# Encoder layer in fp32 on one core: merged products taken by pairs, cached rows on GpSimd's queue, a written order for the first up products, last hidden rows kept in the ring tiles, and new places in SBUF for the operands

## The chip, the core and the metric

The kernel runs on one core of a Trainium2 chip. The metric is the device time of one execution in microseconds, lower is better. The five engines are named as the profile names them: PE (TensorE, its weight loads shown as PEld), DVE (VectorE), ACT (ScalarE), POOL (GpSimd) and SP (SyncE). SP does nothing but start DMAs; POOL starts DMAs too, on a queue of its own.

## What is computed

One inference step of a one-layer encoder, all in fp32, for 1024 new frames and 64 frames of a running stream with 512 cached key and value rows (1088 tokens of 1024 features together).

```python
def mixer(xn, ...):
    cb, cc, ch, q, k, v, ga, gb = jnp.split(xn @ w_in, splits, axis=-1)   # 1024 -> 5120
    cv, conv_state = causal_conv(cc * ch, conv_prefix, w_conv)           # width 3
    ya = (cb * cv) @ w_conv_out                                          # 512 -> 1024
    o, new_k, new_v = attn_fn(heads(q), heads(k), heads(v))              # 8 heads of 64, own chunk + 8 before
    yb = o.reshape(B, L, ATT_DIM) @ w_attn_out                           # 512 -> 1024
    merged = jax.nn.sigmoid(ga) * ya + jax.nn.sigmoid(gb) * yb
    return merged @ w_out, conv_state, new_k, new_v                      # 1024 -> 1024

def trunk(x, ...):
    x = x + mixer(rmsnorm(x, g_mix), ...)
    x = x + (silu(xf @ w_ff1) * (xf @ w_ff3)) @ w_ff2    # xf = rmsnorm(x, g_ffn); 1024 -> 2816 -> 1024
    return rmsnorm(x, g_final), conv_state, new_k, new_v
```

Outputs are the two y, the new convolution states, and the key and value caches, of which `cache_k_sample` and `cache_v_sample` are the old cache moved up by 64 rows with the 64 new rows behind.

## The kernel before

**Products.** Every fp32 operand is split into a high and a low part in the type fp32r: ACT casts the high part, DVE subtracts it from the source to get the low part (`split`, lines 122 and 123). A product is then three matmuls into one PSUM bank: high weight by high data, high weight by low data, low weight by high data. Tokens are two halves of 544 (`HT`), each taken in two pieces of 272 columns (`HN`).

**Seven products for a 2x2 block.** The input projections for q, k, the convolution (cc, ch, cb) and half of gb, and the FFN's up projections, run in units of 256 output columns (`Unit`, `run`). A unit replaces the eight block products of a 2x2 by 2x2 block product by seven, in the order of `STEPS` (1, 2, 6, 7, 5, 4, 3), each 24 matmuls of 128x272 on line 240. Steps 1, 2, 4, 3 use a quarter of the normalized tokens (tiles `xn`, later `mg`), steps 6, 7, 5 use sums of quarters (tiles `xs`, later `tt`). The weights' sums are made on DVE (line 197). Two units run interleaved with each other, step by step: `run` is a generator, and after each step it prepares a later unit's weights.

**Stages, in order of time.** (1) Load, RMSNorm and transpose the tokens tile by tile; V is projected on the way (lines 475 to 477, tokens as weights, 512 columns moving). (2) Projection units to 300 us or so. The epilogues run on ACT and DVE and use one big scratch tile `scr`, cut by hand into slots that are handed out in turn (`slot(STAGE, ...)`, `slot(CC, ...)`, `slot(UT, ...)`). `cc_done` and its inner `whole` (line 543) add a unit's parts out of PSUM, `summed` (line 551) does so for the others. `cache_load` brings cached k and v rows to `scr`, and `cache_tile` stores them back into the sample caches, splits v into `v_d` (`put_v`), and transposes k. `bias_tables` (lines 117 and 118) copies a table through a `STAGE` slot. (3) Gates ga and gb (lines 302 to 304 of `product`), with the attention's heads woven in between; `gate` copies the result to a tile `gst` (line 779) and POOL stores it to DRAM (line 780). (4) For each of eight blocks m of 128 output rows: `ya` from the tile `u` and `yb` from the tile `ob`, each 48 matmuls; `ob` is made from the attention's output at the same time (line 1015 multiplies by the row factor, then `split`). (5) Output projection w_out (lines 1084 to 1089), RMSNorm, transposes (line 1153) and the sums `tt` (`second_half`, line 1179). (6) 22 up units a0, b0, a1, b1 and so on, with SiLU and the product in `hidden_done`; `keep` splits seven forms of a hidden block into a tile `hq` and POOL stores it to `h_d` (line 1245). (7) Down projection (line 1526): hidden rows come back as weights (`ht`), w_ff2 lies split in seven `ring` tiles and is the 512 columns wide moving operand. (8) Final norm and the stores.

**What sets the order.** A tile framework schedules each engine's instruction list ahead of time from the program and from estimated costs; `tc.issue_after(x)` keeps what is written in its block behind instruction x. On the chip each engine takes its list strictly in order.

**Where operands lie.** Tiles are placed one behind the other in each partition of SBUF, so sizes decide places. Before, a token tile is `[P, 2, 4, HT]`: all four high blocks, then all four low ones. Worked out from the sizes, the 272 columns wide moving operands start 32 bytes past a multiple of 64 in `xn`, `mg` and `tt` (6000 matmuls) and on a multiple of 64 in `xs`, `u` and `ob` (1632). The weights of all of them start 224 bytes past a multiple of 256.

Of the kernel before, what the change touches and what calls it, by code (L numbers as in the profile page):

```python
# [15 lines left out]
P = 128  # L16
# [22 lines left out]
WARM = 14  # L39


class Quarters:
# [23 lines left out]
def encoder_kernel(ctx: ExitStack, tc: tile.TileContext, ins, outs):  # L66
# [11 lines left out]
    mspool = ctx.enter_context(tc.tile_pool(name="mspool", bufs=1, reuse_waits="tile", side="right"))  # L78
    ws = ctx.enter_context(tc.tile_pool(name="ws", bufs=8, reuse_waits="tile", side="right"))
# [33 lines left out]
    def bias_tables(j, t):  # L113

        t = t.rearrange("p (h n) -> p h n", h=2)
        src = ins["bias_ext"][2 * j, 384:]
        nc.sync.dma_start(t, bass.AP(tensor=src.tensor, offset=src.offset, ap=[[0, P], [768, 2], [1, 384]]))
        nc.sync.dma_start(bias_d[2 * j : 2 * j + 2].rearrange("h (p n) -> p h n", n=384), t)

    def split(hi, lo, src):  # L120

        a = act.copy(hi, src)  # L122
        vec.tensor_tensor(lo, src, hi.bitcast(F32), op=ALU.subtract)  # L123
        return a.ins
# [4 lines left out]

    def quarters(nm):  # L130
        return Quarters(
            {gh: apool.tile([P, 2, 4, HT], F32R, tag=f"o{p}", name=f"{nm}{gh[0]}{gh[1]}") for p, gh in PLAIN.items()}
        )

    def three_sums(pool, nm):
        return {p: pool.tile([P, 2, 4, HT], F32R, tag=f"o{p}", name=f"{nm}{p}") for p in (6, 7, 5)}

    def both(t, c, n, src):
        split(t[:, 0, :, c : c + n], t[:, 1, :, c : c + n], src)
# [36 lines left out]
    class Unit:  # L176
# [9 lines left out]
        def plain(self, p, src):  # L186
            self.w[p] = [
                ws.tile([P, 4, P], F32R, tag=t, name=f"{t}{self.nm}_{p}") for t in ("wh", "wl")
            ]
            split(*self.w[p], src)  # L190
# [28 lines left out]

    def run(unit, x, banks, snaps, done, ahead):  # L220
# [10 lines left out]
        for si, p in enumerate(STEPS):  # L231
# [5 lines left out]
            for k in range(4):  # L237
                for n, (w, l) in enumerate(((hi, 0), (hi, 1), (lo, 0))):
                    for j in range(2):
                        mm(  # L240
                            t[:, j, :HN], w[:, k, :], x[p][:, l, k, j * HN : (j + 1) * HN],
                            start=p in (1, 2, 7) and k == 0 and n == 0,
                            stop=k == 3 and n == 2, skip_group_check=p in (6, 5, 4, 3),
                        )
# [30 lines left out]
    def prep(upto):  # L275
        while prep.n < min(upto, len(plan)):
# [3 lines left out]
            for k in range(0, kt, 4):  # L280
                hi, lo = (ws.tile([P, 4, P], F32R, tag=t, name=f"{t}p{prep.n}_{k}") for t in ("wh", "wl"))
# [31 lines left out]
    for m in range(0, 8, 2):  # L313
        lds = [{"src": ins[nm][0][:, m * P : (m + 2) * P], "w": 2 * P} for nm in ("w_conv_out", "w_attn_out")]
        plan += [(ld, 4, j * P) for j in range(2) for ld in lds]
# [7 lines left out]
    t1 = three_sums(t1_pool, "xs")  # L323

    scr = t1_pool.tile([P, 11496], F32, name="scr")
    X, GM, SUMS, KEPT, VST, SQ, FEW = (0, 1024, 9312), 2048, 3072, (4096, 5120), (6144, 7168), 8192, 9264
    V32 = [10336, 10848]
    SNAP, STAGE, CC, UT = [544 * i for i in range(5)], [2720, 3808, 9312, 10400], [4896, 5988], [7080, 8172]
    turn = {}
# [43 lines left out]
    def split_wv(half, behind=None):  # L373
        for k in range(4):
            hi, lo = (ws.tile([P, 512], F32R, tag=t, name=f"{t}v{half}_{k}") for t in ("wh", "wl"))
# [28 lines left out]


# [32 lines left out]
    def right_half(src, c, n):  # L438
        for g in range(2):
# [3 lines left out]
            xn.t[0, 1][:, :, :, c : c + n].rearrange("p l k t -> p (l k) t").bitcast(F32),  # L443
# [56 lines left out]
    warm = bank1("A", "warm")  # L500
    ones = mspool.tile([P, 2, 512], F32R, tag="ms", name="ones")[:, 0]
    act.copy(ones, cols[:, 13:14].to_broadcast([P, 512]))
    for n in range(WARM):
        mm(warm[:, n % 2], ones[:, :P], ones, start=True, stop=True)
# [3 lines left out]
    split_wv(0, mixed[0])  # L508
    split_wv(1, mixed[0])
# [105 lines left out]
    ccs, uts = ([scr[:, a : a + L] for a in places] for places in (CC, UT))  # L615
# [65 lines left out]
    def cache_load(i):  # L681
        cts[i] = ct = slot(UT, 2 * ATT)
        nc.sync.dma_start(ct[:, :ATT], ck[i * P : (i + 1) * P])
        nc.sync.dma_start(ct[:, ATT:], cvv[i * P : (i + 1) * P])

    def cache_tile(i):
        ct = cts[i]
        a = 0 if i else TS
        row = i * P + a - TS
        for nm, o in (("k", 0), ("v", ATT)):  # L690
            nc.gpsimd.dma_start(outs[f"cache_{nm}_sample"][row : row + P - a], ct[a:, o : o + ATT])
# [33 lines left out]
    for n in range(len(units)):  # L725
        if n in (4, 5):
            for j in range(2):
                bias_tables(2 * (n - 4) + j, slot(STAGE, 768))
# [35 lines left out]
    st_pool = pg_stack.enter_context(tc.tile_pool(name="st_pool", bufs=2, reuse_waits="tile"))  # L764
# [210 lines left out]
    def gates_in(m):  # L975
        sg = {}
        for o, n in PIECES:
            for nm, src in (("ga", ga_d), ("gb", gb_d)):
                t = sg[nm, o] = mp.tile([P, HN], F32, tag=nm, name=f"{nm}{m}_{o}")
                nc.sync.dma_start(t, src[m * P : (m + 1) * P, o : o + n])  # L980
        return sg
# [3 lines left out]
    nc.sync.dma_start(xn.t[0, 1].rearrange("p l k t -> p (l k) t").bitcast(F32), x21_d)  # L985
# [7 lines left out]
    for i in range(4, len(GATES)):  # L993
        gate_w[i] = next_w()
        if i == len(GATES) - LAST:
# [4 lines left out]
            u = Acts(uo.tile([P, 2, 4, T], F32R, name="u"))  # L1000
            ob = Acts(uo.tile([P, 2, 4, T], F32R, name="ob"))
            mp = pg_stack.enter_context(tc.tile_pool(name="mgp", bufs=4, reuse_waits="tile"))
            sg = gates_in(0)
            for k in range(4):
                nc.sync.dma_start(u.t[:, :, k].bitcast(F32), u_d[k])
            for k in range(4):
                o = ob.t[:, 0, k].bitcast(F32)
                nc.sync.dma_start(o, o_d[k * P : (k + 1) * P])
                r = mp.tile([P, T], F32, tag="rc", name=f"rc{k}", bufs=2)
                for j in range(2):  # L1010
                    src = rc_d[2 * k + j]
                    nc.sync.dma_start(
# [3 lines left out]
                split(ob.t[:, 0, k], ob.t[:, 1, k], r)  # L1016
        for c in range(4):
# [7 lines left out]
    for m in range(8):  # L1025
        wa, wb = next_w(), next_w()
        if m:
            sg = gates_in(m)
        for o, n in PIECES:
            for nm in ("ga", "gb"):  # L1030
                act.activation(sg[nm, o], sg[nm, o], AF.Sigmoid)
            ya = psum2.tile([P, 512], F32, tag="mm", name=f"ya{m}_{o}")
            product(ya[:, :n], wa, u, o, n)
            vec.tensor_tensor(sg["ga", o], ya[:, :n], sg["ga", o], op=ALU.mult)
        for o, n in PIECES:
            t = sg["ga", o]
            yb = psum2.tile([P, 512], F32, tag="mm", name=f"yb{m}_{o}")
            product(yb[:, :n], wb, ob, o, n)
            vec.tensor_tensor(sg["gb", o], yb[:, :n], sg["gb", o], op=ALU.mult)
            vec.tensor_tensor(t, t, sg["gb", o], op=ALU.add)  # L1040
            split(mg.at(0, m, o, n), mg.at(1, m, o, n), t)
            h, a = o // HT, 512 - o % HT
            if a < n:
                split(ms[:, m, 0, 32 * h : 32 * h + 32], ms[:, m, 1, 32 * h : 32 * h + 32], t[:, a:])
# [16 lines left out]
    def wo_half(hf):  # L1061
        r = []
        for kq in range(2):
# [7 lines left out]
            for k in range(4):  # L1071
                hi = ws.tile([P, 512], F32R, tag="wh", name=f"woh{hf}_{kq}_{k}")
                lo = ws.tile([P, 512], F32R, tag="wl", name=f"wol{hf}_{kq}_{k}")
# [37 lines left out]
    if True:  # L1111
# [17 lines left out]
        def second(i):  # L1129
# [13 lines left out]
            vec.scalar_tensor_tensor(xg[:n], xt[:n], r[:n], gb_row[:n], op0=ALU.mult, op1=ALU.mult)  # L1143
# [26 lines left out]
        rest = []  # L1170

        def second_half(src, c, n):
# [8 lines left out]
            def others():  # L1181
                minus(f[:, 0], s[:, 1], f[:, 0])
                both(tt[7], c, n, f[:, 0])
                both(tt[5], c, n, s[:, 0])
# [424 lines left out]
```

## Time and profile before

| | |
|---|---|
| median of three runs | 1498.62 us (1498.4 to 1502.81) |
| the profiled execution: time, span | 1501.25 us, 1499.5 us |
| mean granted TensorE clock | 0.999 |
| PE busy | 1472.1 us, 98% of the span, 10192 matmuls |
| DVE, ACT, POOL busy | 980.9 us, 682.1 us, 128.8 us |
| DMA over the span | 264.73 MB, 177 GB/s in the mean |

The page gives a share of busy time by engine, the busy tenths of 40 slices of the span, the DMA queues, the chain of work that ended last and the costliest groups of instructions by line. PE is at 9 tenths or more in all slices but the first and the last. A matmul's own duration in the records (some 290 ns for 272 columns) is longer than its distance to the next one, since they are pipelined; the chain of waits gives a run of matmuls as one piece, from which the distance follows. The notes in brackets of a timeline row give the idle time of that engine ahead of the row and what ended it.

### The profile page before, as it was taken

The page shows a single profiled execution, that of the slowest core. Times are in us where ns is not written, and L with a number is a line of the kernel's source. Part 1 is how long each engine was busy: PE and PEld are TensorE (multiplying, and loading weights), DVE is VectorE, ACT ScalarE, POOL GpSimd, SP SyncE. Part 2 cuts the span into 40 slices and gives each one's busy share as a digit, 9 for nine tenths or more (in the row PEclk, how much of TensorE's full clock was granted, in tenths as well). Part 3 has the DMA queues.
Part 4 walks back from the last instruction along what each step waited for, and adds up shares of the span by engine and source line. Part 5 has one row for each costly group of instructions (what it writes and reads, how often), then busy time and mean ns, then how long its engine had stood idle before and what let it go on. Part 6 is the DMA issues. An engine that isn't in the chain of part 4 may idle for free.

```text
span 1499.5 us, 26494 instructions
## 1 busy us (share of the span) xinstructions
PE 1472.1 (98%) x10192; PEld 1380.2 (92%) x10192; DVE 980.9 (65%) x1852; ACT 682.1 (45%) x1398; POOL 128.8 (9%) x236
## 2 busy tenths in 40 slices
PE   8999999999999999999999999999999999999997
PEld 6899999999999998998889999999999999788886
DVE  7975466633776743863489676666666668757577
ACT  7654333334776662541356444444444445403123
POOL 1300010001111111000000111100011011000000
PEclk9999999999999999999999999999999999999999
DMA  8696613178776538655432444433344438767675
GB/s 288 188 313 215 194 54 122 58 216 220 189 191 179 144 94 278 185 150 170 151 113 78 144 142 148 149 139 117 118 154 147 156 141 309 250 231 233 229 262 204
DMA packets 167518, 264.73 MB, mean 177 GB/s; under 512 B 19008, under 2 KB 103168, under 8 KB 167264
## 3 DMA queue, kind: packets, MB, share of 16 engines
q1 hardware_dynamic: 146736, 198.23, 42.7%
q0 software_dynamic: 19504, 62.71, 11.5%
q10 hardware_dynamic: 1152, 2.10, 0.4%
q8 instruction: 80, 1.31, 0.4%
q14 instruction: 46, 0.38, 0.1%
HBM read 171.06 MB, written 91.92 MB: 175 GB/s over the span
## 4 chain that ended last, share of the span: by engine, by line
issue 44%; PE 43%; POOL 4%; DMA 4%; DVE 3%; ACT 1%; SPq 1%; POOLq 0%; ACTq 0%; DVEq 0%
PE A L1526 7%; PE D L1526 3%; POOL h_d L1245 3%; PE B L1526 2%; PE t L918 2%; PE Acb L240 2%; PE Ach L240 2%; PE Ak L240 2%; PE g L302 2%; PE g L303 2%; PE Agb L240 2%; PE g L304 2%; PE pv L943 1%; PE Aq L240 1%; PE s L871 1%
## 5 line engine op out<-in xcount | busy, mean ns | idle before, releaser
L1526 PE MATMUL A<-ring,ht 128*128 128x512 f32 x528 | 124.6, 390 | 1.7 <-ACT acc L1536 1.1
L1526 PEld LDWEIGHTS A<-ring,ht 128*128 128x128 f32 x528 | 98.8, 188 | 23.3 <-ACT acc L1536 1.5
L302 PE MATMUL g<-xn,whp 128*128 128x272 f32 x384 | 113.0, 294 | 0.9 <-ACT gst L779 0.9
L303 PE MATMUL g<-xn,whp 128*128 128x272 f32 x384 | 111.8, 291 | 0.0
L304 PE MATMUL g<-xn,wlp 128*128 128x272 f32 x384 | 111.1, 289 | 0.0
L122 ACT CAST ring<-w2r 128x512 fp32r<-128x512 f32 (+1 forms) x78 | 43.4, 587 | 99.9 <-PE A L1526 50.7
L122 ACT CAST hq<-sa 128x512 fp32r<-128x512 f32 x77 | 47.7, 620 | 88.0 <-DVE sa L1257 54.1
L1245 POOL DMA_DIRECT2D h_d<-hq x77 | 41.0, 532 | 417.2 <-DVE hq L123 216.3
L123 DVE TENSOR_TENSOR hq<-sa,hq 128x512 fp32r<-128x512 f32 x77 | 53.2, 691 | 36.0 <-ACT hq L122 35.8
L829 DVE CUSTOM_DVE_ANT_0 p<-s,bb 128x640 f32<-128x640 f32 (+5 forms) x72 | 47.5, 661 | 43.2 <-DMA qd<-q_d 28.1
L302 PEld LDWEIGHTS g<-xn,whp 128*128 128x128 f32 x384 | 72.3, 188 | 2.1 <-ACT gst L779 1.1
L304 PEld LDWEIGHTS g<-xn,wlp 128*128 128x128 f32 x384 | 72.3, 188 | 0.5
L303 PEld LDWEIGHTS g<-xn,whp 128*128 128x128 f32 x384 | 72.4, 189 | 0.3
L123 DVE TENSOR_TENSOR wla<-rawa,wha 128x512 fp32r<-128x512 f32 x56 | 38.5, 688 | 40.5 <-ACT wha L122 40.5
L240 PE MATMUL Aa<-tt,wha 128*128 128x272 f32 x352 | 59.1, 289 | 3.7 <-ACT tt L122 2.5
L1526 PE MATMUL D<-ring,ht 128*128 128x512 f32 x264 | 62.6, 389 | 0.0
L1526 PEld LDWEIGHTS D<-ring,ht 128*128 128x128 f32 x264 | 49.6, 188 | 10.3
L240 PE MATMUL Ab<-mg,whb 128*128 128x272 f32 x352 | 58.4, 288 | 0.0
L240 PE MATMUL Aa<-mg,wha 128*128 128x272 f32 x352 | 58.3, 288 | 0.0
L240 PE MATMUL Ab<-tt,whb 128*128 128x272 f32 x352 | 58.3, 288 | 0.0
L122 ACT CAST wha<-rawa 128x512 fp32r<-128x512 f32 x56 | 34.8, 621 | 51.3 <-PE Ab L240 35.5
L123 DVE TENSOR_TENSOR ring<-w2r,ring 128x512 fp32r<-128x512 f32 (+1 forms) x78 | 48.7, 649 | 12.0 <-ACT ring L122 12.0
(522 smaller groups left out, 4369.8 us busy)
## 6 DMA issues: line engine op xcount, KB each, us to landing
h_d<-hq POOLq DMA_DIRECT2D x77, 512.0 KB, 3.7
ht<-h_d SPq DMA_DIRECT2D x154, 256.0 KB, 3.7
w2r<-in_w_ff SPq DMA_DIRECT2D x11, 1024.0 KB, 5.6
rawa<-in_w_ff SPq DMA_DIRECT2D x11, 1024.0 KB, 5.8
rawb<-in_w_ff SPq DMA_DIRECT2D x11, 1024.0 KB, 5.4
qd<-q_d SPq DMA_DIRECT2D x32, 272.0 KB, 4.8
rawp<-in_w_in SPq DMA_DIRECT2D x6, 1024.0 KB, 6.6
u_d<-scr SPq DMA_DIRECT2D x8, 544.0 KB, 5.3
```

The lines of the kernel that those rows point to most:

```text
L122: a = act.copy(hi, src)
L123: vec.tensor_tensor(lo, src, hi.bitcast(F32), op=ALU.subtract)
L240: mm(t[:, j, :HN], w[:, k, :], x[p][:, l, k, j * HN : (j + 1) * HN], start=p in (1, 2, 7) and k == 0 and n == 0, stop=k == 3 and n == 2, s ...
L302: mm(out, a, p, start=k == 0, stop=False)
L303: mm(out, a, q, start=False, stop=False)
L304: mm(out, b, p, start=False, stop=k == kt - 1)
L829: vec.tensor_tensor_reduce(out=s if len(ps.shape) == 2 else s.rearrange("p (a b) -> p a b", a=2), in0=ps, in1=bias if len(ps.shape) == 2 e ...
L871: mm(ps[:r, i, :w], q[0][:, q0 : q0 + r], k[:, ksl], start=True, stop=False)
L918: nc.tensor.transpose(tp[:, i * P : (i + 1) * P], s[:, i * P : (i + 1) * P], ident)
L943: mm(pv[:, :, lo:hi], v[:, kb, :], pt[:, :, kb - base, lo:hi], start=i == 0, stop=i == len(blocks) - 1,)
L1245: nc.gpsimd.dma_start(h_d[p, c - 1], hq.rearrange("p i l t -> p (i l t)").bitcast(F32))
L1526: mm(t, ht[k][:, j, x], w[:, l], start=p in (1, 2, 7) and k == 0 and n == 0, stop=k == len(ks) - 1 and n == 2, skip_group_check=p in (6, 5 ...
```

## The change

1. **Layout.** `Quarters.at`, `operand` and `both`: a token tile now holds for each block k its high and low part side by side (`[P, 4, 2, HT]`), in a place of 4416 words. `pair` and `moving_pair` make weight tiles of two sizes, 512 and 576 words, and take the low part (for the wide moving ones the high part) at an offset inside the larger. Small tiles (`gap`, `lead1`, `lead2`) shift what lies behind them. `ring` tiles start 16 words into their place. After it, all 272 columns wide moving operands start 32 bytes past a multiple of 64, high weights 32 bytes past a multiple of 256, low weights on a multiple of 256. Of the 512 columns wide matmuls, 1368 of 1656 had operand and weight at the same place within 256 bytes before and 1248 of 1656 after.
2. **Warm-up.** The 14 warming matmuls are written ahead of the first loads' norm; 8 more transposes follow the first token tile.
3. **Cached rows.** `cache_load` starts its DMAs from POOL. The copies of old cache rows out of `scr` are gone; two DMAs copy 448 rows of each cache from DRAM to DRAM (917,504 bytes each), from POOL, waiting for nothing.
4. **Projections.** `CC` has a third slot and `STAGE` one less; the tables' loads and stores are written one unit apart.
5. **Gates and merged products.** `st_pool` has five buffers for two. Blocks m are taken in pairs: ya of m and m+1, then yb of m and m+1. gb rows come in one load of 128x1088 for four of 128x272, the row factors `rc` have three buffers for two.
6. **Up products.** The last two tiles' transposes, the sums and casts of `second_half`, the weights of a0 and the waiting SiLU are given an order with `issue_after`.
7. **Last hidden rows.** Of the last hidden block, forms 7, 5, 6 and 3 are split into the last quarter of ring tiles 1, 2, 6 and 7, which are not in use yet, and no longer into `hq`, of which there are three buffers.

Three places in the instruction lists follow. The first is DVE about 175 us into the program: `rawgb` is the raw weight block of the first gb unit, `Acc` the PSUM tile of the first cc unit, `sf` a scratch tile for weight sums. Before:

```order
L197 TENSOR_TENSOR sf_724<-rawgb_1987 128x512
L197 TENSOR_TENSOR sf_724<-sf_724,rawgb_1987 128x512
L630 MEMSET scr 128x2
L197 TENSOR_TENSOR rawgb_1987<-rawgb_1987 128x4x128
L543 TENSOR_TENSOR scr<-Acc_1763,scr 128x544
L123 TENSOR_TENSOR wlch_4_1950<-rawch_1761,whch_4_1949 128x512
```

After:

```order
L655 MEMSET scr 128x2
L568 TENSOR_TENSOR scr<-Acc_1766,scr 128x544
L130 TENSOR_TENSOR wlch_4_1953<-rawch_1764,whch_4_1952 128x512
L216 TENSOR_TENSOR sf_737<-rawgb_1990 128x512
L216 TENSOR_TENSOR sf_737<-sf_737,rawgb_1990 128x512
L216 TENSOR_TENSOR rawgb_1990<-rawgb_1990 128x4x128
```

The three sums of raw gb weights stood ahead of the reading of `Acc` and now stand behind it.

The second is PE at the start of the up products: `xt_6` and `xt_7` are the transposes of the last two token tiles, `Aa`, `Ba`, `Ab`, `Bb` the PSUM tiles of the units a0 and b0, and `tt` the sums tile of step 6. Before:

```order
L240 MATMUL Ab_9171<-mg_6963,whb_1_9163 128x272 x4
L240 MATMUL Ab_9171<-mg_6963,wlb_1_9164 128x272 x2
L1153 MATMUL xt_7_9198<-ident,xg_7_9071 128x128 x8
L240 MATMUL Aa_9092<-tt_8266,wha_6_9267 128x272 x3
L240 MATMUL Bb_9214<-mg_6964,whb_2_9167 128x272 x4
L240 MATMUL Bb_9214<-mg_6964,wlb_2_9168 128x272 x2
```

After, from the transposes of tile 7 on and then from the end of step 2 of b0 on:

```order
L261 MATMUL Ab_9144<-mg_6971,whb_1_9136 128x272
L1197 MATMUL xt_7_9120<-ident,xg_7_9029 128x128 x8
L261 MATMUL Ab_9144<-mg_6971,whb_1_9136 128x272 x3
...
L261 MATMUL Bb_9171<-mg_6972,wlb_2_9141 128x272 x2
L261 MATMUL Aa_9050<-tt_8224,wha_6_9199 128x272 x4
L261 MATMUL Aa_9050<-tt_8224,wla_6_9200 128x272 x2
```

Step 6 of a0 stood right behind the transposes of tile 7, ahead of step 2 of b0; it now stands behind all of b0's steps 1 and 2, and tile 7 is transposed some 17 matmuls earlier in b0's step 1.

The third is the start of POOL's list; `ident` is the identity for the transposes, `x_d` and `v_d` are tensors in DRAM. Before:

```order
masks.py:197 MEMSET ident 128x128
masks.py:199 ISA
masks.py:199 AFFINE_SELECT ident<-ident 128x128
L441 DMA x_d<-xn_95 1024x1x32
L344 DMA v_d<-scr 64x8x128
```

After:

```order
masks.py:197 MEMSET ident 128x128
L1504 DMA out_cache_k_sample<-in_cache_k 16x14336
masks.py:199 ISA
masks.py:199 AFFINE_SELECT ident<-ident 128x128
L1504 DMA out_cache_v_sample<-in_cache_v 16x14336
L469 DMA x_d<-xn_99 1024x1x32
```

The two copies of old cache rows, written into the loop over the up units, stand first among POOL's DMAs.

The core of the diff:

```diff
-        return self.t[k // 4, h][:, l, k % 4, o - h * HT : o - h * HT + n]
+        return self.t[k // 4, h][:, k % 4, l, o - h * HT : o - h * HT + n]
...
+    gap.tile([P, 48], F32, name="gap")
...
+    def operand(pool, p, nm, place=PLACE):
+        t = pool.tile([P, place], F32R, tag=f"o{p}", name=nm)
+        return t[:, : 8 * HT].rearrange("p (k l n) -> p k l n", k=4, l=2)
+
+    def pair(nm):
+        hi = ws.tile([P, 4, P], F32R, tag="wh", name=f"wh{nm}")
+        lo = ws.tile([P, WIDE], F32R, tag="wl", name=f"wl{nm}")
+        return hi, lo[:, 56:568].rearrange("p (k n) -> p k n", k=4)
+
+    def moving_pair(nm):
+        hi = ws.tile([P, WIDE], F32R, tag="wl", name=f"wh{nm}")
+        lo = ws.tile([P, 512], F32R, tag="wh", name=f"wl{nm}")
+        return hi[:, 48:560], lo
...
-    SNAP, STAGE, CC, UT = [544 * i for i in range(5)], [2720, 3808, 9312, 10400], [4896, 5988], [7080, 8172]
-    turn = {}
+    SNAP, STAGE, CC, UT = [544 * i for i in range(5)], [2720, 3808, 9264], [4896, 5988, 10352], [7080, 8172]
+    turn = {tuple(CC): 1}
...
-        nc.sync.dma_start(ct[:, :ATT], ck[i * P : (i + 1) * P])
-        nc.sync.dma_start(ct[:, ATT:], cvv[i * P : (i + 1) * P])
+        nc.gpsimd.dma_start(ct[:, :ATT], ck[i * P : (i + 1) * P])
+        nc.gpsimd.dma_start(ct[:, ATT:], cvv[i * P : (i + 1) * P])
...
-        for nm, o in (("k", 0), ("v", ATT)):
-            nc.gpsimd.dma_start(outs[f"cache_{nm}_sample"][row : row + P - a], ct[a:, o : o + ATT])
...
-    st_pool = pg_stack.enter_context(tc.tile_pool(name="st_pool", bufs=2, reuse_waits="tile"))
+    st_pool = pg_stack.enter_context(tc.tile_pool(name="st_pool", bufs=5, reuse_waits="tile"))
...
-                r = mp.tile([P, T], F32, tag="rc", name=f"rc{k}", bufs=2)
+                r = mp.tile([P, T], F32, tag="rc", name=f"rc{k}", bufs=3)
...
+    for m0 in range(0, 8, 2):
+        for m in (m0, m0 + 1):
+            wa = next_w()
...
+                product(ya[:, :n], wa, u, o, n)
+                vec.tensor_tensor(t, ya[:, :n], t, op=ALU.mult)
+        for m in (m0, m0 + 1):
+            wb = next_w()
...
+                product(yb[:, :n], wb, ob, o, n)
...
+            if p == NF // 2 - 1 and c in LATE:
+                hq = ring_of(LATE[c])[:, 3072:4096].rearrange("p (i l t) -> p i l t", i=4, l=2)
+            else:
+                hq = hp.tile([P, 4, 2, P], F32R, tag="hq", name=f"hq{p}_{c}", bufs=3)
...
-            ring[p] = pool.tile([P, 8 * HT], F32R, tag=f"o{p}", name=f"ring{p}")
+            ring[p] = pool.tile([P, PLACE], F32R, tag=f"o{p}", name=f"ring{p}")[:, 16 : 16 + 8 * HT]
...
+    with tc.issue_after(normed2[-1]):
+        u0.prep(2)
+    with tc.issue_after(urgent[0]), tc.issue_after(urgent[1]):
+        for forms, st in zip(zip(*rest), (3, 4, 5)):
+            for form in forms:
+                form()
+            u0.prep(st)
...
+    with tc.issue_after(newest[0]):
+        for _ in r0:
+            pass
...
+        if n == 4:
+            for nm, src in (("k", ck), ("v", cvv)):
+                nc.gpsimd.dma_start(outs[f"cache_{nm}_sample"][: CACHE - TS], src[TS:])
```

More of the change, by code (lines that the diff above doesn't have):

```diff
@@ L186, in plain @@
         def plain(self, p, src):
[L187 to L190, printed above, removed]
+            self.w[p] = pair(f"{self.nm}_{p}")
+            self.cast = split(*self.w[p], src)[0]
         def prep(self, step):
@@ L507, in encoder_kernel @@
     turned1(ORDER[0])
-    split_wv(0, mixed[0])
-    split_wv(1, mixed[0])
+    for n in range(WARM[1]):
+        nc.tensor.transpose(warm[:, 0, :P], ident, ident)
+    split_wv(0, mixed[0][0])
+    split_wv(1, mixed[0][0])
     for n, i in enumerate(ORDER):
@@ L1403, in encoder_kernel @@
     next(r0)
+    turned(*late.pop(0), "BD")
     next(r0)
```

201 lines of the change are left out of this document (114 added, 87 removed).

## The prediction

> **What bounds the kernel now.** I read the page's busy times and its 40 slices first, then PE's waits, then the chain of waits and the timelines around each wait.
>
> ```profile
> PE 1472.1 (98%) x10192; PEld 1380.2 (92%) x10192; DVE 980.9 (65%) x1852; ACT 682.1 (45%) x1398; POOL 128.8 (9%) x236
> PE   8999999999999999999999999999999999999997
> ```
>
> TensorE's matmuls fill 98% of the span from the first slices to the last. So a change can do two things only: shorten what PE waits for, or shorten the distance between matmuls. What the other engines do counts where PE stands still for it. The list of PE's waits says how much there is:
>
> ```profile
> PE warm L504 <- ACT ones L502: 2.9, 1, 2.9
> PE Aa L240 <- ACT tt L122: 2.5, 2, 1.4
> PE Acc L240 <- DVE scr L543: 2.3, 1, 2.3
> PE yb L302 <- ACT ob L122: 1.9, 2, 1.4
> PE Aq L240 <- DVE scr L551: 1.3, 1, 1.3
> PE pvv L475 <- ACT whv L122: 1.2, 1, 1.2
> PE Aa L240 <- ACT sa_Q L228: 1.2, 2, 0.6
> PE A L1526 <- ACT acc L1536: 1.1, 1, 1.1
> ...
> PE g L302 <- ACT gst L779: 0.9, 1, 0.9
> ...
> PE A L1526 <- DVE acc L1538: 0.6, 1, 0.6
> PE yb L303 <- DVE ob L123: 0.6, 1, 0.6
> ```
>
> Columns are total us, times and the longest. Seven of these eleven rows stand at places that the change touches. Everything else is the stream itself, of which the chain gives the distance between matmuls (start, us, what):
>
> ```profile
> 182.80 3.01 PE Ach L240 x24
> 188.81 2.98 PE Ach L240 x24
> 191.79 2.99 PE Dch L240 x24
> 1303.39 6.80 PE A L1526 x30
> ```
>
> 24 products of 272 columns take 3.01 us, 125.4 ns each; 30 of 512 columns take 6.80 us, 226.7 ns each. The 240 more columns cost 101.3 ns, 0.422 ns a column, at which 272 columns are 114.8 ns. Some 10.6 ns of each product are therefore not columns. Line 240 has 34 units of 7 steps of 24, 5712 products; lines 302 to 304 have 160 blocks k in 4 pieces of 3, 1920 (12 gates of 8 blocks, 16 merged rows of 4). Of these 7632 one nanosecond of distance is 7.6 us.
>
> **The change part by part: waits.** All terms are against the profiled execution (1501.25 us, span 1499.5), which is 2.63 us above the median.
>
> *Value rows, −1.3.* PE's wait for `scr` L551 goes back to a slot of `CC`:
>
> ```profile
> 101.22 7.36 DMA v_d<-scr
> 108.60 0.62 ACT L122 CAST scr<-scr 128x512 fp32r<-128x512 f32 x1 [4.74 <-DMA v_d<-scr]
> ```
>
> ACT stands 4.74 us at the head of its list for a store of v rows to land before the slot is free, and q's epilogue is queued behind it. A third slot takes that store off the path. The cached rows themselves now come from POOL's queue, and I see no late one: a load waits there for a slot of `UT` as before.
>
> *Raw gb weights, −2.3.*
>
> ```profile
> 166.73 9.97 DMA rawgb<-in_w_in
> 176.79 0.69 DVE L197 TENSOR_TENSOR sf<-rawgb 128x512 f32<-128x512 f32 x1 [4.46 <-DMA rawgb<-in_w_in]
> 178.74 0.72 DVE L543 TENSOR_TENSOR scr<-Acc,scr 128x544 f32<-128x544 f32 x1
> 179.51 3.29 PE Acc L240 x24
> ```
>
> DVE waited 4.46 us for the load and then did three sums before it read `Acc` at 178.74. In the new order `Acc` is read first, and the sums' consumer is gb0, which PE reaches after ch's steps, some ten steps of 3 us later. On SP the load now stands behind more stores; if it comes 3 us later, that slack covers it.
>
> *Gates and merged products, −3.4.* A gate waits 0.9 for `gst`, and yb waits 1.9 + 0.6 for `ob`:
>
> ```profile
> 580.50 0.39 ACT L779 COPY gst<-g 128x272 f32<-128x272 f32 x1 [7.37 <-DMA gb_d<-gst]
> 580.60 1.29 DVE L1015 TENSOR_TENSOR rc<-ob,rc 128x1088 f32<-128x1088 f32 x1 [17.89 <-DMA ob<-o_d]
> 597.33 1.10 ACT L122 CAST ob<-rc 128x1088 fp32r<-128x1088 f32 x1 [4.29 <-DVE rc L1015]
> 598.46 1.29 DVE L123 TENSOR_TENSOR ob<-rc,ob 128x1088 fp32r<-128x1088 f32 x1 [1.17 <-ACT ob L122]
> ```
>
> ACT stood 7.37 us for `gst` stores with two buffers; five cover that. The last block of `ob` is done at 599.75. Taking ya of block 1 before yb of block 0 puts 48 products, 6.0 us, in front of yb, and the third `rc` buffer lets the last load start earlier. The stalls were 2.5, so 6.0 covers them with 3.5 to spare.
>
> *First up products, −2.5 and +0.7.*
>
> ```profile
> 797.16 1.06 PE L1153 MATMUL xt<-ident,xg 128*128 128x128 f32 x8
> 799.61 0.39 PE L240 MATMUL Aa<-tt,wha 128*128 128x272 f32 x1 [1.38 <-ACT tt L122]
> 801.12 0.52 PE L240 MATMUL Aa<-tt,wha 128*128 128x272 f32 x2 [1.12 <-ACT tt L122]
> ```
>
> Step 6 came 1.3 us behind the transposes that its data come from. Tile 7 now goes 17 products (2.1 us) earlier and step 2 of b0 (3.0 us) stands in between, more than the 2.5 lost. The next user is step 7: its `tt` is cast by DVE behind the addition that waits for the end of b0's step 2, and I count DVE done about 0.7 us after PE has finished step 6.
>
> *Last hidden rows, −1.7.* PE's waits on L1526, 1.1 + 0.6, come at 1278 to 1283, where ACT and DVE are late with `acc`; they are late since ACT stood 2.56 and 1.57 us for `hq` buffers shortly before:
>
> ```profile
> 1264.63 0.62 ACT L122 CAST hq<-sa 128x512 fp32r<-128x512 f32 x1 [2.56 <-DMA h_d<-hq]
> 1266.81 0.62 ACT L122 CAST hq<-sa 128x512 fp32r<-128x512 f32 x1 [1.57 <-DMA h_d<-hq]
> ```
>
> Four places in the ring tiles take these casts, so the 4.1 us of ACT are free, more than twice what PE lost. Together the waits give −1.3 −2.3 −3.4 −1.8 −1.7 = **−10.5**. They could give half of that if each is replaced by the next thing that is late.
>
> **The start, +3.0.** The two copies of old cache rows need nothing and stand first among POOL's DMAs, 1.84 MB together. Before, this stretch is full already; the DMA view of the first 8 us (40 slices of 0.2 us) and the timelines:
>
> ```profile
> GB/s 0 0 0 0 0 0 0 0 0 0 184 82 102 225 389 389 307 102 307 266 328 287 328 369 430 307 430 369 389 410 355 117 86 24 2 41 82 20 61 205
> 7.35 1.06 ACT L388 ACTIVATE scr<-scr 128x1024 f32<-128x1024 f32 x1 [1.22 <-DMA scr<-in_x_prompt]
> 10.56 0.45 PE L475 MATMUL pvv<-whv,xs 128*64 128x512 f32 x1 [1.20 <-ACT whv L122]
> 12.28 0.44 PE L476 MATMUL pvv<-wlv,xs 128*64 128x512 f32 x1 [0.38 <-DVE wlv L123]
> ```
>
> Tokens and weights come just in time: ACT waits 1.22 us for the first prompt tile, and PE then waits for the split of the V weights. From 10.56 on PE is the bound, so whatever the loads lose is added to the end. At the 400 GB/s that the busiest slices reach, 1.84 MB are 4.6 us of all 16 DMA engines. Between 6.2 and 7.8 us the engines move little, and that gap can swallow some 1.5 us of it: +3.0 is my value, nothing to +4.6 the bounds. Later the copies of old rows out of `scr` are gone from POOL, which was 9% busy and is no bound: nothing.
>
> **Places in SBUF, −6.1.** No row of before shows the new places, but rows show that places matter. The step of 24 products takes 3.01 us on quarters (starting 32 past a multiple of 64) and 2.98 to 2.99 on sums (on a multiple of 64; weights the same), some 0.8 ns a product. Mean records of one 512 columns wide shape differ more:
>
> ```profile
> L1526 PE MATMUL A<-ring,ht 128*128 128x512 f32 x528 | 124.6, 390 | 1.7 <-ACT acc L1536 1.1
> L1084 PE MATMUL wo<-woh,mg 128*128 128x512 f32 x128 | 51.0, 398 | 0.0
> ```
>
> With the low weights on a multiple of 256 a third of the new products have operand and weight 32 bytes apart, as the sums had; with high and low parts side by side the pattern is the same in every block. The nearest row is 0.8 ns, and I take it for all 7632: −6.1. The small end is a loss: the 1632 products that had the 0.8 lose it (+1.3) and the 924 down products of line 1526 lose at most the 8 ns between these two rows (+7). The far end is the 10.6 ns that are not columns, −81 at most. The 512 columns wide ones I leave at nothing, since nearly as many as before share a place with their weights.
>
> The Trainium skill ("SBUF — State Buffer", section "SBUF: two separate sides") speaks against this term: PE never waits on anyone for SBUF, only DVE and GpSimd share a port. By that rule the term would be nothing. The 390 and 398 ns of one shape do not show who caused the difference, so the rule stays as a rival.
>
> Sum: −10.5 + 3.0 − 6.1 = −13.6 on 1501.25, 1487.6; less the 2.63 that the profiled run was above the median: **1485**.
>
> **The rivals.** *Distance unchanged:* the fixed 10.6 ns belong to the product and its weight load, whatever the addresses. For it: quarters and sums, on different tiles, lie within 1% of 125 ns in the rows above. Against it: the 0.8 ns above. Only waits and start count, −7.5: 1491.
>
> *Distance falls:* the low weights' place or the side by side parts take 2 to 5 ns off each 272 columns product. For it: 10.6 ns are there to be had, and nearly every product changes its place against its weights. Against it: the only row with other places shows 0.8. 2 to 5 ns are −15 to −38; with −7.5 this gives 1453 to 1476. The 2 is twice the row and the 5 half of the 10.6.
>
> The Trainium skill ("TensorE: Matmul & The Clock Gate", section "Wait — 56ns, not 53.3ns?") gives columns at 2.4 GHz and about 2.5 ns as the distance of back-to-back matmuls, 115.8 ns here. The trace has 125.4 and disagrees by 9.6; by the page alone, an estimate, this rival would go as far as −73.
>
> *Slower, by the new places:* the stream reads and the next weights' load meet more often where both start 32 past a multiple of 64, which two thirds of the products now do, `u`, `ob`, `xs` and the down products among them. The price is 7.6 us a nanosecond; from +1.0 ns on the waits' gain is used up, and at +2 ns, a quarter of the 8 ns by which wo and down differ, the time is 1499 − 7.5 + 15 = 1506. Against it: the 32-and-32 case is what 6000 products have already.
>
> *The waits are only moved:* `rawgb` late behind SP's stores, step 7 of a0 waiting for its `tt`, gb's single load late for yb. If half of the waits come back and the start costs its 4.6, and the distance stays, −5.2 + 4.6 is about nothing: 1498.
>
> **How the numbers follow.** Forecast (1478 to 1490): 0.40. Distance unchanged (1489 to 1494): 0.20. Distance falls: 0.20. Waits only moved: 0.08. Slower by places: 0.12. About 0.3%, 4.5 us, is what a measurement of this kernel can tell from no change. Faster by more: 0.40 + 0.20 + 0.19 and a little of the moved waits, 0.80. Within: 0.09. Slower: 0.11. The range leaves out the far half of the falling distance (below 1462) and the slower case beyond 1501.
>
> **What would show it.** Each wait by its row: no `v_d` wait on ACT near 105, `Acc` starting right behind the step before it, no wait on L302's yb and g, no 2.5 at the first `tt` products and at most 0.7 at the second, no waits at the first down products. The start: the first V product at 10.56 or up to 4.6 later. The places: 24 products on line 261 in 3.01, 2.99 or less. If that piece reads 2.95 or 3.05, the forecast is wrong by some 19 us to one side or the other, and nothing else in the list is as large.

## The result, and the profile after

The changed kernel takes 1508.36 us (median of ten runs, 1502.21 to 1512.1) against 1500.0 (ten runs of before beside it, 1495.89 to 1505.82): a ratio of 1.0046, 95% interval 1.003 to 1.0063. It is 0.5% slower; 1485 was forecast. The profiled execution took 1509.5 us, its span is 1507.7, the mean granted clock 0.992 instead of 0.999.

PE's waits in the changed kernel (total us, times, longest):

```profile
PE pvv L503 <- ACT whv L129: 6.9, 1, 6.9
PE xt L445 <- issue: 3.5, 1, 3.5
PE warm L432 <- ACT ones L430: 2.9, 1, 2.9
PE Dq L261 <- ACT scr L249: 2.5, 1, 2.5
PE Aa L261 <- ACT sa_Q L249: 2.1, 3, 1.0
PE A L1599 <- DVE acc L1611: 1.6, 1, 1.6
PE A L1599 <- ACT acc L1609: 1.1, 1, 1.1
PE g L323 <- ACT scr L566: 1.0, 1, 1.0
PE yb L324 <- DVE ob L130: 0.9, 1, 0.9
PE yb L323 <- ACT ob L129: 0.8, 1, 0.8
```

Of the waits that the prediction wanted gone, those for `Acc`, for `gst` and at `Aa` for `tt` are gone. Those of yb for `ob` (1.7 us) and at the first down products (3.2 on `acc`) are not. Two rows are new at the very top, and they stand ahead of the first V product. The starts of the stages, read from the timelines of the two traces and of the first run told below, show where the time went:

| first matmul of | before | after | first run | after less before |
|---|---|---|---|---|
| V | 10.56 | 22.54 | 10.92 | +12.0 |
| q | 68.48 | 81.43 | 68.42 | +13.0 |
| k | 113.74 | 129.31 | 112.70 | +15.6 |
| gb | 203.61 | 216.94 | 200.26 | +13.3 |
| gates | 329.49 | 344.63 | 326.82 | +15.1 |
| ya | 584.04 | 596.55 | 578.93 | +12.5 |
| w_out | 683.48 | 696.28 | 674.92 | +12.8 |
| up | 787.11 | 798.65 | 777.30 | +11.5 |
| down | 1256.93 | 1263.04 | 1244.46 | +6.1 |
| the span's end | 1499.5 | 1507.7 | 1489.2 | +8.2 |

13 us are lost before q, and the rest of the kernel wins back 4.8. The timeline of ACT and then of PE at the start of the changed kernel shows what is waited for:

```profile
12.71 1.06 ACT L410 ACTIVATE scr<-scr 128x1024 f32<-128x1024 f32 x1 [6.66 <-DMA scr<-in_x_prompt]
19.79 1.06 ACT L410 ACTIVATE scr<-scr 128x1024 f32<-128x1024 f32 x1 [5.50 <-DMA scr<-in_x_prompt]
...
21.87 0.62 ACT L129 CAST whv<-wv 128x512 fp32r<-128x512 f32 x1
```

```profile
12.46 1.30 PE L445 MATMUL xt<-ident,scr 64*128 64x64 f32 x8 [3.52 <-issue]
13.70 1.97 PE L532 MATMUL warm<-ident 128*128 128x128 f32 x8
```

The second token tile's squares (before at 7.35) come at 12.71, since its load is late. Then ACT stands 5.50 us more for the third tile, and only behind that tile come the casts that V waits for. The order had changed on ACT as well. In the kernel before, the first `whv` casts come ahead of the third tile's squares, which stand 15 rows further down, behind all eight of these casts:

```profile
9.89 1.14 ACT L122 CAST whv<-wv 128x512 fp32r<-128x512 f32 x2
...
15.69 1.10 ACT L388 ACTIVATE scr<-scr 128x1024 f32<-128x1024 f32 x1
```

PE's 3.52 us ahead of the first transposes go back to a load too: DVE stands 4.95 us for `g_mix`. The DMA view of the first 24 us of the changed kernel gives packets, megabytes and share of the engines' time by queue (q1 is SP's, q0 POOL's), and in the last column the us from issue to landing:

```profile
q1 hardware_dynamic: 1888, 4.46, 55.2%
q0 software_dynamic: 64, 1.84, 19.8%
...
out_cache_k_sample<-in_cache_k POOLq DMA_DIRECT2D x1, 896.0 KB, 6.6
out_cache_v_sample<-in_cache_v POOLq DMA_DIRECT2D x1, 896.0 KB, 9.0
scr<-in_g_mix SPq DMA_DIRECT2D x1, 512.0 KB, 10.1
```

Before:

```profile
scr<-in_g_mix SPq DMA_DIRECT2D x1, 512.0 KB, 4.3
```

The two copies move 1.84 MB in 64 packets, 28.7 KB each, beside SP's 2.4 KB packets; `g_mix` takes 10.1 us to land instead of 4.3. The Trainium skill ("DMA: Bandwidth & Descriptors", "Queues, rings and completion order") has each DMA engine change between queues only at the end of a packet; that agrees with small loads being held up for about as long as the copies last.

### The profile page after: what moved, and what is told of

The parts are those of the page before. It is cut to its first block, busy times and chain, and to the rows that moved or that the text cites. A ratio compares the mean times of both kernels' runs of the same rounds, so it can differ in the third digit from the quotient of the medians.

```text
span 1507.7 us, 26462 instructions
## 1 busy us (share of the span) xinstructions
PE 1474.0 (98%) x10200; PEld 1381.5 (92%) x10200; DVE 982.1 (65%) x1852; ACT 681.2 (45%) x1398; POOL 130.0 (9%) x238
## 3 DMA queue, kind: packets, MB, share of 16 engines
q0 software_dynamic: 19632, 64.81, 11.9%
## 4 chain that ended last, share of the span: by engine, by line
PE 55%; issue 33%; DVE 4%; DMA 3%; POOL 3%; ACT 1%; SPq 0%; POOLq 0%; ACTq 0%; DVEq 0%
PE A L1599 7%; PE D L1599 3%; PE Aa L261 3%; PE Ab L261 2%; PE g L323 2%; PE g L324 2%; PE g L325 2%; PE B L1599 2%; PE t L942 2%; PE Ak L261 2%; PE Ach L261 2%; PE Acb L261 2%; PE pv L967 2%; PE Acc L261 2%; PE Agb L261 2%
```

## The experiments

Times are medians, with the ratio to the kernel before, measured beside each run, and its 95% interval. The kernel before had 1501.7 us beside runs 1 to 4, 1499.8 beside runs 5 to 8 and 1498.7 beside run 11.

**1. The copies held until the up stage.**

```diff
-            nc.gpsimd.dma_start(h_d[p, c - 1], ...)
+            stored[0] = nc.gpsimd.dma_start(h_d[p, c - 1], ...).ins
...
         if n == 4:
+            with tc.issue_after(stored[0]):
                 for nm, src in (("k", ck), ("v", cvv)):
```

> The changed kernel with the two cache copies held behind the stores of the fourth up block on POOL's queue. In the trace of the changed kernel the first V product starts at 22.5 us against 10.6 before, and 13.0 us are lost by the end of V. If the two copies at the start are the cause of all of it, the first V product is back near 10.6 and the time falls by 12 to 13 us, to about 1496, some 4 us under the kernel before. Rival: the start is late for another reason (the warm-up written earlier, 8 more transposes, the cast order); then the time stays within 3 us of 1508. Late copies could also disturb the up stage: then a wait appears near 830 to 850 us.

1488.62 us, 0.9907 (0.9888 to 0.9925): 13 us faster than before and about 20 faster than the changed kernel. On ACT the casts stand ahead of the third tile's squares again, with nothing done for it, so it was the scheduler that had moved them in answer to the copies; by which estimate is not shown. The first V product is at 10.92. PE's waits in this run:

```profile
PE A L1603 <- DVE acc L1615: 1.6, 1, 1.6
PE Aa L262 <- ACT sa_Q L250: 1.5, 3, 0.8
PE A L1603 <- ACT acc L1613: 1.1, 1, 1.1
PE D L1603 <- ACT acc L1613: 0.9, 1, 0.9
```

The gain of 19.7 us is more than the 13 expected. Three later waits of the changed kernel are gone too (`Dq` 2.5, g 1.0, yb 1.7). By the starts of the stages they had cost 3.6, 1.1 and 3.8, and behind two of them the granted clock was low (start and end of the stretch, its length, PE's busy time and count, clock, DMA share, GB/s; the changed kernel):

```profile
121.40:124.40 3.00, 2.99 (x13) 0.50 0.62 180
612.00:616.00 4.00, 4.00 (x20) 0.57 0.80 278
```

Behind the wait of 2.3 us for `Acc` in the kernel before it was 1.00 (179.4 to 183 us), so not every such wait has this price. Against this the changed kernel was 2.8 us faster from up to down, of which run 4 tells more. That the copies cause the loss at the start is shown by the undoing; the rival (the warm-up) is out. That they cause the three later waits is not shown: run 11, with the copies late, has one of 1.4 us at `Dq`. The late copies disturb nothing that can be seen.

**2. Copies early, ACT's order as before.**

```diff
-                    split(hi, lo, wv_raw[half][:, k])
+                    casts.append(split(hi, lo, wv_raw[half][:, k])[0])
...
+        if n == 0:
+            with tc.issue_after(casts[-1]):
+                normed(ORDER[n + 2])
-        if n + 2 < len(ORDER):
+        elif n + 2 < len(ORDER):
             normed(ORDER[n + 2])
```

> The changed kernel with the copies at the start as they are, but the third token tile's squares on ACT put behind the casts of the V weights, as the kernel before has it. If the loss at the start has two parts, DMA sharing and ACT standing for the third tile ahead of the V casts (21.9 us for the first cast, 19.8 for the third tile), the first V product comes at 16 to 18 and the time falls by 4 to 6, to about 1503. Rival: sharing alone sets the start (the V weights themselves land that late): no change, 1508.

1500.46 us, 0.9983 (0.9968 to 0.9998), 8 us under the changed kernel by the medians. The first V product:

```profile
15.56 0.69 PE L505 MATMUL pvv<-whv,xs 128*64 128x512 f32 x1
```

The delay of V has two parts: 22.54 − 15.56 = 7.0 us is ACT's order while the third tile is late, 15.56 − 10.56 = 5.0 the sharing of the DMA engines. The rival is out. But the sharing costs more than its 5.0: by the medians this run is 11.8 us over the first run (9.2 by the spans). Its q comes 6.0 us later than there and its k 9.9. In between PE stands 2.5 us at `Aq` for DVE, and its clock is 0.64 and 0.51 in the four microseconds behind; whether that wait belongs to the copies is open.

**3. The kernel before with the copies alone.**

```diff
...
-        for nm, o in (("k", 0), ("v", ATT)):
-            nc.gpsimd.dma_start(outs[f"cache_{nm}_sample"][row : row + P - a], ct[a:, o : o + ATT])
...
+        if n == 4:
+            for nm, src in (("k", ck), ("v", cvv)):
+                nc.gpsimd.dma_start(outs[f"cache_{nm}_sample"][: CACHE - TS], src[TS:])
```

> The kernel before with one part of the change alone: its stores of old cache rows out of scratch are replaced by the two DRAM to DRAM copies, which come to stand first on POOL; ACT's list gets the third tile's squares ahead of the V casts too. If the copies are the whole loss at the start, the first V product comes at about 22 and the time is 12 to 13 us over before, 1512. Rival (the warm-up and the 8 transposes matter): less than 8 us.

1516.54 us, 1.0086 (1.006 to 1.0113): 14.8 us slower by the medians, from one part alone. In its trace q starts 14.1 us late: 11.9 at the first V product, and 2.2 more up to q, with a granted clock of 0.50 from 12 to 28 us. The first V product waits as in the changed kernel:

```profile
22.48 0.69 PE L475 MATMUL pvv<-whv,xs 128*64 128x512 f32 x1 [4.41 <-ACT whv L122]
```

**4. All of the layout undone, copies late** (`[P, 2, 4, HT]` again, 512 words for all weight tiles, no shifts).

> The kernel of the first run with all of the layout undone: high blocks ahead of low ones again, no shifts, weight and ring tiles at their old sizes. In the trace of the changed kernel the distance of up products is 124.05 ns against 125.3, that of first projections 0.3 to 1.3 ns more on the sums. If the places cause this, the up products are at 125.3 again and the time is 4 to 5 us over that of the first run. Rival: the distance follows from the order of the work and not from places: within 1 us of the first run.

1491.1 us, 0.9929 (0.9908 to 0.995), against 1488.6 with the layout; the intervals overlap, the profiled spans are 1489.3 and 1489.2. The expected 4 to 5 us did not come. From up to down this run takes 468.6 us against the first run's 467.2, from q to the gates 257.2 against 258.4, so the layout won 1.4 and lost 1.2. The 124.05 ns of the changed kernel's up stage are therefore not a fixed rate of the layout. Matmuls in stretches of 100 us of the up stage show why (columns as in run 1; the count is in brackets). Before, the changed kernel, and the first run:

```profile
850.00:950.00 100.00, 100.00 (x800) 1.00 0.37 130
```

```profile
850.00:950.00 100.00, 100.00 (x814) 1.00 0.41 148
1000.00:1100.00 100.00, 100.00 (x798) 1.00 0.39 139
1110.00:1210.00 100.00, 100.00 (x813) 1.00 0.38 135
```

```profile
850.00:950.00 100.00, 100.00 (x799) 1.00 0.42 146
1000.00:1100.00 100.00, 99.64 (x795) 1.00 0.39 139
1110.00:1210.00 100.00, 100.00 (x813) 1.00 0.42 152
```

The same places give 798 or 814 products in 100 us (the 795 have a wait among them). The rate holds between two waits for `sa_Q` (at 982 and 1109 in the changed kernel, at 1089 in the first run) and may be the other after one.

**5. Last hidden rows in `hq` again, copies late** (`LATE = {}`).

> The first run's kernel with the last hidden rows cast into hq again and not into the ring tiles. In the first run PE waits 4.1 us at the first down products (1263.9, 1268.5, 1272.6), against 2.0 in the kernel before; there the load of the next w_ff2 rows is issued 7.6 us after the first down product against 6.9 before and lands late. If the ring places cause this, the three waits shrink to 2.0 and the time falls by 2, to 1486.5. Rival: the waits come with the order of the up work or the places and stay: no change. Second rival, my prediction's: the ring places save time, so it rises by 1.7.

1487.58 us, 0.9912 (0.9899 to 0.9925): not told apart from the first run. By the lists of waits, PE waits 3.0 us at the first down products (1.6, 1.1, 0.3) against 3.6 in the first run and 1.7 in the kernel before (the expectation had 4.1 and 2.0), and 2.6 in run 3, which has the rows in `hq` and the order of before. DVE's timeline of the first run shows what replaced ACT's wait there:

```profile
1262.14 0.69 DVE L1402 TENSOR_TENSOR w2r<-w2r 128x512 f32<-128x512 f32 x1 [4.15 <-DMA w2r<-in_w_ff]
```

There ACT does not stand for `hq`, and DVE stands 4.15 us for the next w_ff2 rows, with the reading of `acc` queued behind. In run 5 it is the other way round: ACT stands 2.67 and 2.99 us for `hq`, and PE's waits are nearly the same. The ring places neither gain nor lose what the median can show. Why PE's wait is 2.6 to 3.6 in these runs and 1.7 in the trace of before stays open.

**6. Side by side alone**, on the old places (`PLACE = 8 * HT, WIDE = 512`, no shifts), and **7. shifts alone** (high blocks ahead of low, the sizes and shifts kept), copies late in both.

> The first run's kernel with high and low parts side by side, but all operands on their old places within 256 bytes (no shifts, old sizes). In the traces so far each step of 24 up products takes 3007 ns with the old layout; with the new layout it takes either 2960 or 3013 ns and keeps one of the two until the stream is next interrupted. If the shifts make the two rates, this run shows one rate near 3007 in the up stage and 2987 on the sums of the projections. Rival: side by side parts make them; then two rates are seen here.

> The first run's kernel with all shifts and sizes, but the four high blocks ahead of the four low ones. If the shifts make the two rates, steps of 2960 and of 3013 ns are seen in the up stage here and 3013 on the sums of the projections. Rival: they need the side by side parts; then one rate, whichever. Time within 5 us of the first run either way.

1492.36 us, 0.9945 (0.9932 to 0.9958), and 1488.63, 0.9923 (0.9909 to 0.9937). The first two stretches, side by side alone and then shifts alone:

```profile
850.00:950.00 100.00, 100.00 (x799) 1.00 0.43 150
1000.00:1100.00 100.00, 100.00 (x798) 1.00 0.39 139
```

```profile
850.00:950.00 100.00, 100.00 (x806) 1.00 0.42 148
1000.00:1100.00 100.00, 100.00 (x805) 1.00 0.40 144
```

Each alone has one rate: 799 and 806, in the third stretch too. Only both together have two. The expectation for run 6 was off by little (3013 ns a step, not 3007), that for run 7 wrong: neither part alone makes two rates. The shifts alone have a steady gain in the up stage: 465.3 us up to down here and 464.5 in run 11, against 468.6 to 471.0 in the three traces with the old places (before, runs 3 and 4). The medians of whole runs do not tell these kernels apart.

**8. No pairs, copies late** (ya of m, then yb of m, `gb` loads and `rc` buffers kept).

> The first run's kernel with the merged products block by block again: ya of m, then yb of m, all else as it is (loads of gb rows in one piece, three rc buffers). In the first run yb does not wait at all, against 3.0 us before. If the pairs are what covers ob, yb waits 2 to 3 us again at its first products and the time rises by that, to 1491. Rival: the third rc buffer and the earlier loads do it alone: no wait, no change.

1489.99 us, 0.9931 (0.9916 to 0.9947), 1.4 over the first run, within the scatter. By the list of waits yb waits 1.4 us in this run's trace (2.5 in before); with pairs nothing in the first run and 1.7 in the changed kernel. From ya to w_out this run takes 98.2 us; the eight traces with pairs take 95.9 to 99.7, six of them 95.9 to 96.5, and before took 99.4. Neither theory is settled: what the pairs gain is some 2 us, and each run shows another wait at yb.

**9. Steps alone.** The kernel leaves the whole computation out (its outputs are zeros).

> Leaves the whole computation out (the outputs are zeros): only steps of 24 matmuls of 128x272 as line 261 has them, without any other engine at work, for 16 combinations of places: high and low parts side by side or blocks of high ahead of low; moving operand, high weights and low weights each starting on a multiple of 64 bytes or 32 past one. Each combination has 6 stretches of 6 steps, with 1 to 6 matmuls of 128x128 ahead of each stretch. If places alone set the rate, and the state is picked by what stands ahead: 3007 ns a step with all three 32 past and blocks of high ahead of low (the kernel before), 2987 when the moving operand is moved by 32, 2987 with the low weights moved (the run with shifts only), 3013 with side by side alone, and both 2960 and 3013 with side by side and low weights moved, depending on the number of matmuls ahead. Rival: the traffic of the other engines makes the rates; then all combinations show one rate here.

The chain of the combination "side by side, low weights moved" has 6 steps to a piece (144 matmuls), with 1 to 6 small ones ahead (the last three pieces are shown; s stands for side by side, o for high blocks ahead of low, then t or z for 32 past a multiple of 64 or on one, of moving operand, high and low weights):

```profile
728.45 18.13 PE s_ttz L86 x144
746.58 0.51 PE s_ttz L81 x5
747.09 17.82 PE s_ttz L86 x144
764.91 0.62 PE s_ttz L81 x6
765.52 18.13 PE s_ttz L86 x144
```

The same matmuls on the same operands take 18.13 us, or 17.82 behind five small ones: steps of 3013 and of 2960 ns, each kept to the end of its piece (a piece has some 50 ns more at its start). With high blocks ahead of low and the low weights moved:

```profile
1612.04 17.99 PE o_ttz L86 x144
1630.03 0.51 PE o_ttz L81 x5
1630.54 17.98 PE o_ttz L86 x144
```

That is 2987 ns a step whatever stands ahead. Five of the 16 combinations have this rate throughout, the others 3003 to 3040 or mixtures. No other engine was at work, so it is the places of PE's own operands, with what stands ahead, that set the rate, and the rival is out. Two expectations failed: with high blocks ahead of low, all three 32 past a multiple of 64 gave 2987, 3013 and 3027 in turn and not 3007, and the moving operand moved gave 3013 and not 2987. So the place within 64 bytes is not all.

**10. Weight places within 256 bytes, steps alone** (outputs again zeros).

> Leaves the whole computation out (the outputs are zeros), as the first run of steps alone: side by side parts with the moving operand 32 past a multiple of 64, high weights at 32, 96, 160 or 224 past a multiple of 256 and low weights at 0, 64, 128 or 192. In that first run this class (low weights on a multiple of 64) was at 3013 ns in five stretches and at 2960 in one. If the place within 64 bytes is all that counts, all 16 combinations here show the same two rates and none is always at 2960. Rival: the place within 256 bytes decides; then one of the 16 is always at 2960, worth 27 ns a step or 6 us in the kernel over places that give 2987.

The combinations differ: with the same places within 64 bytes, two combinations are at 2987 throughout, two at 3000, others at 3013 with pieces of 3000 to 3067, and only the one of the changed kernel shows 2960, in one piece of six, with the very figures of run 9. None is always at 2960, so no kernel was made of it.

**11. Copies late, shifts alone, hidden rows in `hq`.**

> Copies late, shifts with blocks of high ahead of low (2987 ns a step throughout), last hidden rows in hq: the parts of the runs so far that cost nothing or help. With 238 steps at 2987 against a mixture of 2960 and 3013 I expect the time of the hq run within 2 us, 1486 to 1489, and 12 us under the kernel before. If the hidden rows' places do help after all, it is 1 to 2 us over the run with shifts only (1488.6).

1487.62 us, 0.9922 (0.9907 to 0.9937). With runs 1, 5 and 7 this is the best, 0.8 to 0.9% under the kernel before and some 1.3% under the changed one; the four are not told apart.

## Why the prediction was wrong

*The start, +3.0 with +4.6 as the bound: this step failed.* It measured +13.0 at the start of q. The sharing delayed the first V product by 5.0, above the bound. But the step went by POOL's list alone. The scheduler had answered to the copies on another engine: ACT's squares of the third tile stood ahead of the V casts, +7.0, as the first dozen rows of ACT's list show. The last 1.0 lies between the first V product and q, and I put it down to the clock, which no run separates: while PE stood, its granted clock fell (columns as above, for the changed kernel and then for before):

```profile
9.00:12.00 3.00, 0.00 (x0) 0.97 0.84 227
22.00:25.00 3.00, 2.46 (x10) 0.50 0.00 0
```

```profile
9.00:12.00 3.00, 1.70 (x15) 1.00 1.05 406
```

"Whatever the loads lose is added to the end" fell short as well: without ACT's part (run 2) the loss is 6.0 at q and 9.2 at the end, by the spans against the first run.

*The waits, −10.5: near the forecast or better in the first run, but for the last.* In the first run the start is as before, and its column in the table less that of before gives each step: from q to k −1.0 (value rows, −1.3 forecast), from k to gb −2.3 (raw weights, −2.3), from gb to the gates +0.7, over gates and merged blocks −5.9 (−3.4). The 2.5 beyond the forecast there are not accounted for; they are not the places, since run 4 has the same. Over w_out it is −1.2, which was not in the sum; the wait of 0.8 for `ms` there is gone too. From up to down it is −2.7, of which the forecast had −1.8 in the waits. The parts are not all shown to be the causes: in run 3, which has two `CC` slots and of the change the copies alone, the waits in q and for `ms` are gone as well. In the changed kernel itself the waits at `Dq`, g and yb, 5.2 us, took back half of the sum, as the rival "the waits are only moved" has it.

*Last hidden rows, −1.7: wrong.* The first run loses 2.2 from down on. Run 5 shows that the ring places gain nothing and cost at most 0.6 of it; the same rival holds here, and the rest of the 2.2 is open.

*Value rows in the changed kernel.* ACT's wait for `v_d` became one for `k_d`:

```profile
119.71 0.62 ACT L129 CAST scr<-scr 128x512 fp32r<-128x512 f32 x1 [4.39 <-DMA k_d<-scr]
```

PE then stands 2.5 us at `Dq`. In the first run ACT stands 2.94 us at this place and PE 0.2; in run 11, whose start is on time, it is 4.06 and 1.4. So the late start is not the only cause.

*Places, −6.1: a size that has no one value.* In two stretches of three the changed kernel's up stage has 814 and 813 products where before had 800. In the projections it runs at the slower of its two rates, 3.01 on the sums too, where before had 2.99, but for short pieces:

```profile
177.29 2.96 PE Bcc L261 x24
186.97 3.01 PE Acc L261 x24
```

With the same places, runs 5 and 8 have 2.96 in most of the projections, and take 255.1 us from q to the gates against 258.4 in the first run. From up to down the changed kernel won 5.4, the first run 2.7. Undone as a whole (run 4), the layout is worth nothing by the spans and 2.5 us by the medians. The rival "distance unchanged" had a reason that fell: run 9 has no other engine at work, and the step goes from 2960 to 3040 ns with the places of PE's own operands. The Trainium skill's sentence ("SBUF — State Buffer", "SBUF: two separate sides") that PE never waits on anyone is about other engines; it says nothing of this, and no run here speaks against it.

*Without the start*, the sum was −16.6; the first run gave −13.1 by the medians and −10.3 by the spans. The changed kernel itself won 4.8 from q to the end. That its 1488.6 lies in the range of the forecast is luck in part: by the spans the places gave about nothing, the last hidden rows gave nothing, while gates, merged blocks and w_out gave 3.7 more than forecast.

## What to carry to other kernels

A DMA that waits for nothing is issued as early as the scheduler likes, so hold it behind something on its own queue, and after such an edit read the first rows of every engine's list, not only the one that issues it. A large copy at the start costs twice: it holds up small loads, and what the scheduler moves in answer may cost more. Before a gain is put down to where operands lie, count matmuls in several stretches of one trace: a rate that changes behind a wait is not fixed by the layout.

## What was not expected of the hardware

With the same operands at the same places, a stream of 128x272 matmuls ran at 2960 or at 3013 ns for 24, and kept its rate until the next interruption, in the kernel and alone (runs 1 and 9). In run 10, moving weights by multiples of 64 bytes changed the step between 2960 and 3067. What makes this was not tried. A wait of PE can cost more than its length: behind those of 2.5 and 1.7 us in the changed kernel the granted clock was 0.50 and 0.57 for some microseconds, behind one of 2.3 us in the kernel before 1.00.
